# A hybrid decoder layer in split fp32: four plain blocks in place of six ahead of the Strassen pairs, token blocks made on demand, and mixer weights split by a copy and an adding transfer

## The chip, the core and the metric

The kernel runs on one core of a Trainium2 chip. The metric is device time in microseconds of one execution. TensorE (PE in the rows) multiplies, VectorE (DVE) and ScalarE (ACT) work element by element, SyncE (SP) issues plain transfers, and GpSimd (POOL) issues those transfers that add what they bring to what is in the target.

## The reference

One layer on 512 tokens of width 1024: half a step of a SwiGLU network, a mixer (4 retention heads beside 8 heads of block attention), half a step of a second SwiGLU network. All of it is fp32.

```
x = x + 0.5 * swiglu(rms(x, ffn1_norm_w), ffn1_w_gate, ffn1_w_up, ffn1_w_down)
proj = rms(x, mix_norm_w) @ w_in                   # 1024 -> 3584
ret = rms(retention(rope(rq), rope(rk), rv)) * silu(rg) * ret_out_beta
att = rms(moba(rope(rms(aq)), rope(rms(ak)), av)) * att_out_beta
x = x + concatenate([ret, att]) @ w_out
x = x + 0.5 * swiglu(rms(x, ffn2_norm_w), ffn2_w_gate, ffn2_w_up, ffn2_w_down)
swiglu(h, g, u, d) = (silu(h @ g) * (h @ u)) @ d    # 1024 -> 2816 -> 1024
```

## The kernel before

**Split products.** Tokens stand along the free dimension (512 columns). For an fp32 product in fp32r, each operand is split into a first part `h` (rounded to fp32r) and a second part `lo` (what the rounding lost). `mm3` (L396) makes a product of three matmuls, `wh xh + wh xl + wl xh`. `split_w` (L373) brings a weight in tiles of 128x512: a load of 256 KB through SP's queue, a ScalarE copy that makes `h`, and a VectorE subtraction `raw - h` that makes `lo`. Slots for these come from rings: 12 for raw weights, 6 for first parts (`wh`), 6 for second parts (`wl`), 45 for token blocks, 98 in all.

**The networks.** `ffn` (L594) has 22 blocks of 128 hidden columns. The first `EVEN` (6) are plain: per block, gate and up each take 8 x 3 matmuls of 512 columns. The other 16 are made in 8 pairs by `hidden` (L635) through `strassen` (L516): a 2x2 Strassen scheme over two halves of the inner dimension, two output blocks, and two halves of the tokens, with 7 products of 24 matmuls for the gate and 24 for the up part, each one block of 128 weights by 256 columns. A pair needs eight loads for its four quarters, two more loads and four adding transfers for sums of quarters, four VectorE sums, and 14 splits. The down projection has 10 plain blocks and 6 pairs, in the same way.

**Token blocks.** Strassen's moving side is one of seven combinations of token quarters, for each of four pairs of input blocks. `token_blocks` (L471) makes all seven for all pairs at once, ahead of the first Strassen product. The products ask for them in the order 0, 1, 3, 4, 5, 6, 2. `weave` (L574) lets neighbouring pairs overlap in the order of the program.

**The mixer.** `proj(c)` (L758) is one projection of 128 columns out of 20 (two weight tiles, 24 matmuls of 512 columns); `values(g)` (L770) makes values for half of the heads (eight weight tiles, 96 matmuls). Around them stand gates, rope, scores, softmax and norms, all with splits of their own on ScalarE and VectorE. The output projection and the second network follow.

**The order.** Nothing is issued as it is written. `Plan` (L75) notes each operation with its tiles and what it depends on, and then goes through time with a price list: at each moment an engine that is free takes, of its operations that are ready and whose slots are free, the one with the lowest place in the program plus a delay. `DELAYS` (L53) is a list of such delays by part of the mixer. The price list counts 2000 ns for a transfer to land, `DMA_LAT` (L88). The chosen order is then fixed; on the chip each engine runs its own list in order and waits on semaphores. As all goes through one helper, each row below has line 202.

Of the kernel before, what the change touches and what calls it, by code (L numbers as in the profile page):

```python
# [42 lines left out]
EARLY = 6  # L43
WARM = 8

EVEN = 6
HALF = (22 - EVEN) // 2

PLAIN = 10
# [1 line left out]
PAIRED = (22 - PLAIN) // 2  # L51

DELAYS = {  # L53
    "att norm 0": -1252, "att norm 1": 245, "att norm 2": -377, "att norm 3": -1320,
    "att out 0 0": -73, "att out 0 1": -287, "att out 1 0": -333, "att out 1 1": 71,
    "att out 2 0": -358, "att out 2 1": -145, "att out 3 0": -9, "att parts 0": -2592,
    "att parts 1": -1912, "att parts 2": -23, "att parts 3": -314, "att raw 0": 349,
    "att raw 1": -845, "att raw 2": -1954, "att rope 0": -79, "att rope 1": -982,
# [9 lines left out]
    "proj 9": 42, "ret out 1": -203, "ret out 2": 171, "ret out 3": 80, "ret rope 0": -747,  # L68
    "ret rope 1": 30, "ret rope 3": 59, "ret scores 0": 229, "ret scores 1": -861,
    "ret scores 2": 36, "ret scores 3": 123, "values 0": 399, "values 1": 751,  # L70
}
PIECES = {0: 1, 1: 2, 2: 4, 4: 8}

# [1 line left out]
class Plan:  # L75
# [9 lines left out]
           "DVE": {"PE": 260.0, "POOL": 205.0, "DVE": 130.0, "ACT": 130.0},  # L85
           "POOL": {"PE": 260.0, "POOL": 105.0}, "DMA": {}}
    LAT_ANY = {"PE": 200.0, "ACT": 145.0, "DVE": 145.0, "POOL": 100.0, "DMA": 100.0}
    LAT_FREE, DMA_LAT, WINDOW = 290.0, 2000.0, 900  # L88

    class _Engine:  # L90
        def __init__(self, plan, name, real):
# [122 lines left out]
    def _order(self):  # L214
# [25 lines left out]
        while done < n:  # L240
            progress = True
            while progress:
                progress = False
                for e in engines:
                    if busy[e] > t:
                        continue
                    skipped, pick = [], None
                    while ready[e]:
                        p, i = heapq.heappop(ready[e])
                        if i > first + self.WINDOW:  # L250
                            heapq.heappush(ready[e], (p, i))
                            break
                        if at[i] <= t:
                            new = [x for x in ops[i][4] if x not in live]
                            want = {}
                            for x in new:
                                for k in self.tiles[x]:
                                    want[k] = want.get(k, 0) + 1
                            if all(free[k] >= v for k, v in want.items()):
                                pick = i  # L260
                                for x in new:
                                    live.add(x)
                                for k, v in want.items():
                                    free[k] -= v
                                break
                        skipped.append((p, i))
                    for s in skipped:
                        heapq.heappush(ready[e], s)
                    if pick is not None:
                        progress = True  # L270
                        order.append(pick)
                        busy[e] = t + ops[pick][1]
                        if ops[pick][7]:
                            other = "POOL" if e == "DVE" else "DVE"
                            busy[e] += max(0.0, share[other] - t)
                            share[e] = busy[e]
                        end = busy[e] + (self.DMA_LAT if e in ("DMA", "POOL") else 0.0)
                        heapq.heappush(events, (busy[e], -1))
                        heapq.heappush(events, (end, pick))
            if not events:  # L280
                raise RuntimeError(f"stuck at {t}: {len(order)} of {n}: {free}")
            t, i, *x = heapq.heappop(events)
            now = [(i, x)]
            while events and events[0][0] <= t:
                _, i, *x = heapq.heappop(events)
                now.append((i, x))
            for i, x in now:
                done += self._ended(i, x, t, free, over, left, events, succ, at, need, ready)
            while first < n and over[first]:
                first += 1  # L290
# [33 lines left out]
def tile_layer(ctx: ExitStack, tc: tile.TileContext, x_t, cols_in, wg1, wu1, wd1, w_int, w_inn,  # L324
# [22 lines left out]
    def f32(ap):  # L347
        return ap.bitcast(F32)
# [21 lines left out]
            n, k = divmod(at[1], self.each)  # L370
            return self.tiles[n][:, k]

    def split_w(src, shape, pieces=None):  # L373

        each = 512 // shape[2]
        raws, hs, ls = [], [], []
        for a in range(0, shape[1], each):
# [4 lines left out]
                to.append(x)  # L382
            if pieces is None:
                nc.sync.dma_start(raw, src[:, a:a + n])
                nc.scalar.activation(h, raw, AF.Copy)
                nc.vector.tensor_sub(lo, raw, f32(h))
        if pieces is not None:
            def piece(a):
                n, o = a.start // each, slice(a.start % each, a.start % each + a.stop - a.start)
# [78 lines left out]
            nc.vector.tensor_scalar(v, ps, EPS, None, op0=OP.add)  # L468
            self.v, self.r = v, rsqrt(v)

    def token_blocks(pairs, gates=None):  # L471


        res = [[] for _ in range(7)]
        gate = lambda q: setattr(nc, "after", gates and gates[min(q, len(gates) - 1)])
        def negative(n, src, bh, bl, o):
            nc.scalar.activation(bh[:, o], src, AF.Copy, scale=-1.0)
            nc.vector.scalar_tensor_tensor(bl[:, o], src, -1.0, f32(bh[:, o]), op0=OP.mult, op1=OP.subtract)
            res[n].append((bh[:, o], bl[:, o]))

        for q, (one, two) in enumerate(pairs):
            gate(q)
            if q % 2 == 0:
                bh, bl = slot(F32R, use="block"), slot(F32R, use="block")
            negative(0, one[:, :256], bh, bl, slice(256 * (q % 2), 256 * (q % 2) + 256))

        def two_blocks(n, t):
            h, lo = split(t, use="block")
            for i in range(2):
                res[n + i].append((h[:, 256 * i:256 * i + 256], lo[:, 256 * i:256 * i + 256]))  # L490

        for q, (one, two) in enumerate(pairs):
            gate(q)
            h, lo = slot(F32R, use="block"), slot(F32R, use="block")
            nc.scalar.activation(h[:, :256], two[:, :256], AF.Copy)
            nc.vector.tensor_sub(lo[:, :256], two[:, :256], f32(h[:, :256]))
            res[1].append((h[:, :256], lo[:, :256]))
            negative(2, two[:, 256:], h, lo, slice(256, 512))
        later = []
        for q, (one, two) in enumerate(pairs):  # L500
            gate(q)
            t = slot(use="block")
            nc.vector.tensor_sub(t[:, :256], one[:, 256:], one[:, :256])
            nc.vector.tensor_sub(t[:, 256:], two[:, 256:], t[:, :256])
            two_blocks(3, t)
            u = slot(use="block")
            nc.vector.tensor_sub(u[:, :256], one[:, 256:], two[:, 256:])
            nc.vector.tensor_sub(u[:, 256:], two[:, :256], t[:, 256:])
            later.append(u)
        for q, u in enumerate(later):  # L510
            gate(q)
            two_blocks(5, u)
        nc.after = None
        return res

    def strassen(load, units, moving, taken):  # L516

# [76 lines left out]
    def ffn(st, x, wg, wu, wd, nxt, was, first=None, last=False):  # L594
# [30 lines left out]
        for q in range(4):  # L625
# [4 lines left out]
                                               op0=OP.mult, op1=OP.mult)  # L630
                two.append(t)
            pairs.append(two)
        blocks = token_blocks(pairs)

        def hidden(one, two):  # L635
            def load(queue, t, m, i, j):
# [58 lines left out]
                mm3(p, wh[:, fb], wl[:, fb], *parts[fb], fb == 0, fb == PLAIN - 1)  # L695
            nc.vector.scalar_tensor_tensor(y, p, 0.5, y, op0=OP.mult, op1=OP.add)
        units = [(n, k0, 0) for k0, n in ((k, min(4, PAIRED - k)) for k in range(0, PAIRED, 4))]
        blocks = token_blocks([(hs[PLAIN + k], hs[PLAIN + PAIRED + k]) for k in range(PAIRED)])

        def output(db):  # L700
            def load(queue, t, u, i, j):
# [55 lines left out]

    def proj(c):  # L758
        was, nc.part = nc.part, f"proj {c}"
        wh, wl = split_w(w_int[c], (128, 8, 128))  # L760
        p = bank("p")
        for kb in range(KB):
            xh, xl = s2.parts[kb]
            mm3(p, wh[:, kb], wl[:, kb], xh, xl, kb == 0, kb == KB - 1)
        nc.part = was
        return p
# [3 lines left out]
    def values(g):  # L770
# [1 line left out]
        nc.part = f"values {g}"  # L772
        ps = [bank("t") for _ in range(3)] + [bank("o")]
        for c in range(4):
            wh, wl = split_w(w_inn[4 * g + c], (128, 2, 512))
            for a in range(2):
                kb = 2 * c + a
                xh, xl = s2.parts[kb]
# [359 lines left out]
```

## Time and profile before

| | |
|---|---|
| median of 3 runs | 961.61 us (960.72 to 962.21) |
| the profiled execution | 962.12 us, span 960.4 us |
| TensorE, VectorE, ScalarE, POOL busy | 949.8, 740.9, 546.9, 83.7 us |
| plain blocks of network 1, its Strassen pairs, its down projection | to 74, to 238, to 346 us of the span |
| mixer | 346 to 577 us |
| output projection and plain blocks, Strassen pairs and down projection of network 2 | to 680, to the end |

Times in a row are from the start of the span. Busy time of TensorE holds waits that lie under the modelled end of a matmul; its pace (the time of a long run over its matmuls) says more.

### The profile page before, as it was taken

How to read it: one execution, taken by the hardware profiler on the slowest of the kernel's cores; microseconds unless marked ns; L12 is line 12 of the kernel's file. 1: busy time of each engine (PE TensorE's matmuls, PEld its weight loads, DVE VectorE, ACT ScalarE, POOL GpSimd, SP SyncE). 2: the span in 40 equal slices, each digit the busy share in tenths (PEclk: the TensorE clock that was granted, in tenths of full speed). 3: DMA queues.
4: the chain of work that ended last, by engine and by line, in shares of the span. 5: the costliest groups of instructions: out<-in, count | busy, mean ns of one | idle time of the engine just before them, and what ended most of it. 6: DMA issues, size and time to landing. Idle time of an engine off the chain costs nothing.

```text
span 960.4 us, 16972 instructions
## 1 busy us (share of the span) xinstructions
PE 949.8 (99%) x6042; PEld 857.3 (89%) x6042; DVE 740.9 (77%) x1512; ACT 546.9 (57%) x1107; POOL 83.7 (9%) x100
## 2 busy tenths in 40 slices
PE   9999999999999999999999999999999999999998
PEld 5889999999889998888788878888999999988998
DVE  7986777798836884379989998888567789893675
ACT  7544555577334555368987975554455647652341
POOL 0211111110002000000000010001111111000120
PEclk9999999999999999999999999999999999999999
DMA  9937666566438772214405554744677665563581
GB/s 310 285 89 183 182 173 154 144 149 180 157 92 186 218 256 105 64 60 121 158 24 155 173 138 109 248 115 101 155 177 180 161 167 138 154 192 99 127 200 43
DMA packets 89156, 146.95 MB, mean 153 GB/s; under 512 B 10736, under 2 KB 24816, under 8 KB 89072
## 3 DMA queue, kind: packets, MB, share of 16 engines
q1 hardware_dynamic: 75248, 122.80, 40.0%
q0 software_dynamic: 13824, 23.07, 15.1%
q8 instruction: 47, 0.77, 0.3%
q14 instruction: 37, 0.30, 0.1%
HBM read 136.40 MB, written 6.29 MB: 149 GB/s over the span
## 4 chain that ended last, share of the span: by engine, by line
PE 86%; ACT 6%; DVE 4%; DMA 1%; SPq 1%; issue 1%; DVEq 0%; ACTq 0%
PE ps L202 86%; ACT s L202 6%; DVE s L202 4%; SPq L202 1%; DMA s<-in_x_t_dram 1%; DMA s<-in_w_int_dram 0%; DMA s<-s 0%; DVE c L202 0%; DVE ad L202 0%; ACT c L202 0%; DVEq L202 0%; ACTq L202 0%
## 5 line engine op out<-in xcount | busy, mean ns | idle before, releaser
L202 PE MATMUL ps<-s 128*128 128x256 f32 (+2 forms) x5872 | 934.9, 320 | 4.6 <-ACT s L202 2.7
L202 PEld LDWEIGHTS ps<-s 128*128 128x128 f32 x5872 | 837.6, 190 | 88.1 <-ACT s L202 7.3
L202 DVE TENSOR_TENSOR s<-s 128x512 fp32r<-128x512 f32 (+4 forms) x918 | 524.6, 622 | 100.0 <-ACT s L202 94.5
L202 ACT ACTIVATE s<-s 128x512 fp32r<-128x512 f32 (+3 forms) x808 | 420.9, 577 | 268.0 <-DVE s L202 191.8
L202 DVE TENSOR_TENSOR s<-ps,s 128x256 f32<-128x256 f32 (+6 forms) x184 | 91.7, 519 | 47.5 <-PE ps L202 30.1
L202 ACT ACTIVATE s<-ps 128x512 f32<-128x512 f32 (+7 forms) x148 | 75.7, 519 | 80.9 <-PE ps L202 76.5
L202 POOL DMA_DIRECT2D s<-in_wg_dram x32 | 28.0, 875 | 575.2 <-ACT s L202 241.6
L202 DVE SCALAR_TENSOR_TENSOR s<-ps,s 128x256 f32<-128x256 f32 (+1 forms) x72 | 34.8, 483 | 38.6 <-PE ps L202 38.5
L202 POOL DMA_DIRECT2D s<-in_wd_dram x32 | 27.9, 982 | 220.6 <-PE ps L202 144.8
L202 DVE SCALAR_TENSOR_TENSOR s<-s 128x256 fp32r<-128x256 f32 (+1 forms) x70 | 37.2, 537 | 11.7 <-ACT s L202 11.4
L202 DVE SCALAR_TENSOR_TENSOR s<-s,cols 128x512 fp32r<-128x512 f32 (+1 forms) x44 | 32.1, 749 | 6.1 <-ACT s L202 5.9
L202 POOL DMA_DIRECT2D s<-in_wu_dram x32 | 29.4, 919 | 53.1 <-DMA s<-in_wu_dram 27.6
L202 ACT ACTIVATE s<-s,cols 128x512 fp32r<-128x512 f32 x24 | 17.1, 720 | 23.3 <-DVE s L202 21.3
L202 ACT ACTIVATE s<-s,c 128x384 f32<-128x384 f32 (+3 forms) x32 | 20.7, 649 | 1.6 <-DVE c L202 1.5
L202 PE MATMUL ps<-ct,s 128*128 128x128 f32 x100 | 17.3, 278 | 1.3 <-ACT s L202 1.2
L202 PEld LDWEIGHTS ps<-ct,s 128*128 128x128 f32 x100 | 11.8, 140 | 5.5 <-ACT s L202 3.9
L202 DVE CUSTOM_DVE_ANT_0 s<-ps,s 128x384 f32<-128x384 f32 (+3 forms) x32 | 14.8, 485 | 0.5 <-PE ps L202 0.4
L202 ACT ACTIVATE s<-ps,cols 128x512 f32<-128x512 f32 x8 | 5.5, 684 | 16.3 <-PE ps L202 16.3
L202 DVE TENSOR_TENSOR s<-s,ps 128x256 f32<-128x256 f32 x32 | 12.0, 417 | 0.0
L202 PE MATMUL ps<-s,cr 128*128 128x512 f32 x30 | 11.7, 410 | 0.2 <-ACT s L202 0.2
L202 DVE SCALAR_TENSOR_TENSOR s<-ps,c,s 128x128 fp32r<-128x128 f32 (+1 forms) x24 | 8.2, 389 | 1.7 <-ACT s L202 1.7
L202 DVE SCALAR_TENSOR_TENSOR s<-s,ps 128x512 f32<-128x512 f32 x12 | 8.2, 683 | 0.6 <-PE ps L202 0.6
(33 smaller groups left out, 76.9 us busy)
## 6 DMA issues: line engine op xcount, KB each, us to landing
s<-in_wg_dram SPq DMA_DIRECT2D x103, 256.0 KB, 3.5
s<-in_wu_dram SPq DMA_DIRECT2D x103, 256.0 KB, 3.6
s<-in_wd_dram SPq DMA_DIRECT2D x72, 256.0 KB, 3.1
s<-in_w_int_dram SPq DMA_DIRECT2D x40, 256.0 KB, 4.4
s<-in_wg_dram POOLq DMA_DIRECT2D x32, 256.0 KB, 4.8
s<-in_wu_dram POOLq DMA_DIRECT2D x32, 256.0 KB, 5.9
s<-in_wd_dram SPq DMA_DIRECT2D x56, 128.0 KB, 2.8
s<-in_x_t_dram SPq DMA_DIRECT2D x16, 256.0 KB, 4.9
```

Of the source, the lines that this page charges most:

```text
L202: self.ops.append([eng, cost, lambda: fn(*args, **kwargs), deps, tiles, i + self.delay + DELAYS.get(self.part, 0), self.part, shared])
```

## The change

`EVEN` goes from 6 to 4, so each network has 4 plain blocks and 9 Strassen pairs. `TokenBlocks` takes the place of `token_blocks`: it makes a block when a product first indexes it, inside the product's loop and thus behind that product's first weight split in the program. In `proj` and `values`, `split_w` gets `by="copy"`: `h` by a VectorE copy, `lo` by ScalarE as `-h`, and then an adding transfer of the same weight from memory on POOL's queue. `w_out` and the networks keep the old split. The planner prices the landing of a POOL transfer at 3000 ns, and `DELAYS` has new numbers (the first lines are shown).

```diff
-EVEN = 6
+EVEN = 4
 HALF = (22 - EVEN) // 2
...
 DELAYS = {
-    "att norm 0": -1252, "att norm 1": 245, "att norm 2": -377, "att norm 3": -1320,
+    "att norm 0": -2603, "att norm 1": 330, "att norm 2": -243, "att norm 3": 188,
...
-    LAT_FREE, DMA_LAT, WINDOW = 290.0, 2000.0, 900
+    LAT_FREE, DMA_LAT, WINDOW = 290.0, {"DMA": 2000.0, "POOL": 3000.0}, 900
...
-                        end = busy[e] + (self.DMA_LAT if e in ("DMA", "POOL") else 0.0)
+                        end = busy[e] + self.DMA_LAT.get(e, 0.0)
...
-    def split_w(src, shape, pieces=None):
+    def split_w(src, shape, pieces=None, by=None):
...
                 nc.sync.dma_start(raw, src[:, a:a + n])
-                nc.scalar.activation(h, raw, AF.Copy)
-                nc.vector.tensor_sub(lo, raw, f32(h))
+                if by == "copy":
+                    nc.vector.tensor_copy(h, raw)
+                else:
+                    nc.scalar.activation(h, raw, AF.Copy)
+                if by is None:
+                    nc.vector.tensor_sub(lo, raw, f32(h))
+                else:
+                    nc.scalar.activation(lo, f32(h), AF.Copy, scale=-1.0)
+                    nc.gpsimd.dma_start(lo, src[:, a:a + n], accum_op=OP.add)
...
-    def token_blocks(pairs, gates=None):
...
+    class TokenBlocks:
+        def __init__(self, pairs):
+            self.pairs, self.made, self.t, self.two = pairs, {}, [], []
+
+        def __getitem__(self, n):
+            if n not in self.made:
+                self.make(n)
+            return self.made[n]
...
+        def both(self, n, t):
             h, lo = split(t, use="block")
             for i in range(2):
-                res[n + i].append((h[:, 256 * i:256 * i + 256], lo[:, 256 * i:256 * i + 256]))
+                self.made.setdefault(n + i, []).append(tuple(x[:, 256 * i:256 * i + 256] for x in (h, lo)))
+
+        def make(self, n):
+            if n == 0:
+                self.made[0] = []
+                for q, (one, two) in enumerate(self.pairs):
+                    if q % 2 == 0:
+                        tiles = slot(F32R, use="block"), slot(F32R, use="block")
+                    self.made[0].append(self.one(one[:, :256], tiles, 256 * (q % 2), -1.0))
+            elif n in (1, 2):
+                if not self.two:
+                    self.two = [(slot(F32R, use="block"), slot(F32R, use="block")) for _ in self.pairs]
+                self.made[n] = [self.one(two[:, 256 * n - 256:256 * n], tiles, 256 * n - 256, 3.0 - 2 * n)
+                                for tiles, (one, two) in zip(self.two, self.pairs)]
+            elif n in (3, 4):
+                for one, two in self.pairs:
+                    t, u = slot(use="block"), slot(use="block")
+                    nc.vector.tensor_sub(t[:, :256], one[:, 256:], one[:, :256])
+                    nc.vector.tensor_sub(t[:, 256:], two[:, 256:], t[:, :256])
+                    self.both(3, t)
+                    nc.vector.tensor_sub(u[:, :256], one[:, 256:], two[:, 256:])
+                    nc.vector.tensor_sub(u[:, 256:], two[:, :256], t[:, 256:])
+                    self.t.append(u)
+            else:
+                for u in self.t:
+                    self.both(5, u)
...
-        blocks = token_blocks(pairs)
+        blocks = TokenBlocks(pairs)
...
-        blocks = token_blocks([(hs[PLAIN + k], hs[PLAIN + PAIRED + k]) for k in range(PAIRED)])
+        blocks = TokenBlocks([(hs[PLAIN + k], hs[PLAIN + PAIRED + k]) for k in range(PAIRED)])
...
-        wh, wl = split_w(w_int[c], (128, 8, 128))
+        wh, wl = split_w(w_int[c], (128, 8, 128), by="copy")
...
-            wh, wl = split_w(w_inn[4 * g + c], (128, 2, 512))
+            wh, wl = split_w(w_inn[4 * g + c], (128, 2, 512), by="copy")
```

## Rows read from the trace of the kernel before

**Rows 1.** The page: busy time, share, instructions; then transfer rate by slice.

```profile
PE 949.8 (99%) x6042; PEld 857.3 (89%) x6042; DVE 740.9 (77%) x1512; ACT 546.9 (57%) x1107; POOL 83.7 (9%) x100
...
GB/s 310 285 89 183 182 173 154 144 149 180 157 92 186 218 256 105 64 60 121 158 24 155 173 138 109 248 115 101 155 177 180 161 167 138 154 192 99 127 200 43
```

**Rows 2.** TensorE in order of time: start, us, first form's name, count of all.

```profile
24.39 85.81 PE L202 MATMUL ps<-s 128*128 128x512 f32 x519
...
580.71 44.41 PE L202 MATMUL ps<-s 128*128 128x512 f32 x195
...
625.42 74.75 PE L202 MATMUL ps<-s 128*128 128x512 f32 x408
...
699.76 132.88 PE L202 MATMUL ps<-s 128*128 128x256 f32 x1106
```

**Rows 3.** Busy us (instructions) by stretch: PE, PEld, DVE, ACT, POOL; clock; transfer share; GB/s.

```profile
27.30:66.40 39.10, 39.10 (x174) 32.36 (x174) 39.01 (x76) 21.60 (x42) 7.60 (x9) 1.00 0.60 172
74.00:238.00 164.00, 163.31 (x1353) 162.78 (x1353) 130.00 (x253) 97.20 (x190) 22.51 (x26) 1.00 0.64 164
346.00:424.00 78.00, 78.00 (x375) 65.54 (x376) 40.69 (x79) 39.34 (x72) 0.00 (x0) 1.00 0.34 118
424.00:510.00 86.00, 84.33 (x445) 70.02 (x444) 76.90 (x185) 70.96 (x159) 0.00 (x0) 1.00 0.35 107
510.00:577.00 67.00, 65.67 (x350) 54.08 (x349) 64.12 (x164) 55.55 (x129) 3.50 (x4) 1.00 0.53 150
```

**Rows 4.** TensorE's groups of one form from 424 to 577 us.

```profile
L202 PE MATMUL ps<-s 128*128 128x512 f32 x442 | 118.2, 400 | 0.5 <-DVE s L202 0.4
L202 PE MATMUL ps<-s 128*128 128x256 f32 x104 | 20.0, 292 | 0.5 <-DVE s L202 0.3 <-ACT s L202 0.2
L202 PE MATMUL ps<-ct,s 128*128 128x128 f32 x96 | 16.7, 278 | 1.3 <-ACT s L202 1.2
L202 PE MATMUL ps<-s 128*128 128x128 f32 x70 | 12.1, 252 | 0.0
L202 PE MATMUL ps<-s 128*128 128x384 f32 x40 | 11.6, 359 | 0.5 <-ACT s L202 0.3 <-DVE s L202 0.2
L202 PE MATMUL ps<-s,cr 128*128 128x512 f32 x18 | 7.2, 415 | 0.2 <-ACT s L202 0.2
L202 PE MATMUL ps<-cr,s 128*128 128x2 f32 x23 | 2.8, 235 | 0.0
```

**Rows 5.** The chain that ended last, from 424 to 577 us, by line.

```profile
by line: ACT s L202 35.1%; PE ps L202 30.1%; DVE s L202 20.7%; SPq L202 4.1%; issue 3.7%; DMA s<-in_w_int_dram 2.9%; DMA s<-s 1.5%; DVE c L202 0.8%; DVE ad L202 0.8%; ACT c L202 0.5%; DVEq L202 0.1%; ACTq L202 0.0%
```

**Rows 6.** VectorE: four pieces in order of time, and one group of one form.

```profile
46.70 0.42 DVE L202 SCALAR_TENSOR_TENSOR s<-s 128x256 fp32r<-128x256 f32 x1
47.04 0.42 DVE L202 TENSOR_TENSOR s<-s 128x256 fp32r<-128x256 f32 x1
...
617.75 4.30 DVE L202 TENSOR_TENSOR s<-s 128x512 f32<-128x512 f32 x7
...
628.34 0.69 DVE L202 SCALAR_TENSOR_TENSOR s<-s 128x512 f32<-128x512 f32 x1 [1.43 <-ACT s L202]
...
L202 DVE MEMSET idle<- 128x256 uint32 x1 | 0.3, 272 | 0.0
```

**Rows 7.** SP's mixer weight loads after 424 us: first and last of 22.

```profile
424.04 1.05 SPq L202 DMA_DIRECT2D s<-in_w_int_dram  x2
...
505.94 1.80 SPq L202 DMA_DIRECT2D s<-in_w_int_dram  x4
```

**Rows 8.** The page's transfer queues, and POOL's issues with us to landing.

```profile
q1 hardware_dynamic: 75248, 122.80, 40.0%
q0 software_dynamic: 13824, 23.07, 15.1%
...
s<-in_wg_dram POOLq DMA_DIRECT2D x32, 256.0 KB, 4.8
s<-in_wu_dram POOLq DMA_DIRECT2D x32, 256.0 KB, 5.9
```

More of the change, by code (lines that the diff above doesn't have):

```diff
@@ L53 @@
 DELAYS = {
-    "att norm 0": -1252, "att norm 1": 245, "att norm 2": -377, "att norm 3": -1320,
[L55 to L58, printed above, removed]
[9 rows of a table removed]
-    "proj 9": 42, "ret out 1": -203, "ret out 2": 171, "ret out 3": 80, "ret rope 0": -747,
-    "ret rope 1": 30, "ret rope 3": 59, "ret scores 0": 229, "ret scores 1": -861,
-    "ret scores 2": 36, "ret scores 3": 123, "values 0": 399, "values 1": 751,
+    "att norm 0": -2603, "att norm 1": 330, "att norm 2": -243, "att norm 3": 188,
+    "att out 0 0": -554, "att out 0 1": 166, "att out 1 0": 373, "att out 1 1": -807,
+    "att out 2 0": 99, "att out 2 1": -93, "att out 3 0": -2464, "att out 3 1": -87,
+    "att parts 0": -4536, "att parts 1": -2396, "att parts 2": 423, "att parts 3": -347,
+    "att raw 0": 24, "att raw 1": -2777, "att raw 2": -2297, "att raw 3": 362, "att rope 0": -905,
[8 rows of a table added]
+    "proj 7": 255, "proj 8": 71, "ret out 0": 51, "ret out 1": -34, "ret out 2": 77,
+    "ret out 3": -30, "ret rope 0": 177, "ret rope 1": -250, "ret rope 2": 2, "ret rope 3": -234,
+    "ret scores 0": 312, "ret scores 1": -682, "ret scores 2": -8, "ret scores 3": -1191,
+    "values 0": 159, "values 1": 751,
 }
@@ L469, in stats, with one @@
             self.v, self.r = v, rsqrt(v)
-    def token_blocks(pairs, gates=None):
[L474 to L487, printed above, removed]
+    class TokenBlocks:
[5 more added lines that the diff above has]
+            return self.made[n]
+        def one(self, src, tiles, o, sign=1.0):
+            h, lo = (t[:, o:o + 256] for t in tiles)
+            if sign > 0:
+                nc.scalar.activation(h, src, AF.Copy)
+                nc.vector.tensor_sub(lo, src, f32(h))
+            else:
+                nc.scalar.activation(h, src, AF.Copy, scale=-1.0)
+                nc.vector.scalar_tensor_tensor(lo, src, -1.0, f32(h), op0=OP.mult, op1=OP.subtract)
+            return h, lo
+        def both(self, n, t):
@@ L488, in two_blocks @@
             h, lo = split(t, use="block")
             for i in range(2):
-                res[n + i].append((h[:, 256 * i:256 * i + 256], lo[:, 256 * i:256 * i + 256]))
[L492 to L514, printed above, removed]
+                self.made.setdefault(n + i, []).append(tuple(x[:, 256 * i:256 * i + 256] for x in (h, lo)))
[20 more added lines that the diff above has]
+                    self.t.append(u)
+            else:
+                for u in self.t:
+                    self.both(5, u)
```

17 rows, old and new, of the table DELAYS are left out of this document.

## The prediction

> **What bounds the kernel now.** I read the page's table of engines first, then TensorE's and VectorE's instructions in order of time, then busy times by stage, and last the chain of waits and the transfers in the mixer.
>
> The table says TensorE is busy 949.8 of 960.4 us [rows 1]; VectorE is next with 740.9. But ends of matmuls are modelled, so the reader should look at the pace. In one long run of the plain form, 195 matmuls of 512 columns take 44.41 us [rows 2]; less the tail of the last (0.39), that is 44.02 / 194 = 0.227 us each. In one long run of Strassen products, 1106 matmuls of 256 columns take 132.88 us; less a tail of 0.28, that is 0.120 each. Both forms run back to back for tens of microseconds: there TensorE alone sets the time, and what is taken from it is gained in full, as long as nothing else falls behind.
>
> The same rows date the first Strassen product. From 24.39 on, 519 matmuls take 85.81 us [rows 2]. With n plain ones, 0.227 n + 0.120 (519 - n) = 85.5, so n = 217 and the first product starts near 24.4 + 49.3 = 73.7 us. For the second network 408 matmuls in 74.75 us from 625.42 give 238 plain ones and a first product near 679.5.
>
> Only the mixer wastes TensorE time. From 424 to 577 it waits visibly for 1.67 + 1.33 = 3.0 us [rows 3], and more lies under modelled ends. Counting forms there [rows 4]: 460 matmuls of 512 columns at 0.227 are 104.4, 104 of 256 at 0.120 are 12.5, 40 of 384 about 7.0 (half-way), 166 of 128 columns between 11.1 (the line through the two prices) and 19.9 (as for 256), 23 tiny ones at most 2.8. That is 135 to 147 us in 153: 6 to 18 us are lost. VectorE is busy 76.9 of 86 and 64.1 of 67 us there, ScalarE 71.0 and 55.6 [rows 3], and of the chain that ended last 35% is ScalarE, 30% TensorE, 21% VectorE [rows 5]. So both small engines share that bound, ScalarE somewhat more.
>
> **The change part by part.**
>
> **Two plain blocks become one pair**, in each network. Removed: 2 x 48 = 96 matmuls of 512 columns, 96 x 0.2269 = 21.78 us. Added: 7 products x 2 x 4 x 3 = 168 of 256 columns, 168 x 0.1200 = 20.16 us. Gain 1.62 us each, 3.25 us in both networks. This is the firm term: the pace of both forms is measured where nothing else binds. The side costs of one more pair: VectorE loses 8 splits and 6 row operations (14 x 0.602 = 8.4 us, a 512-wide pass being (4.30 - 0.69) / 6 = 0.602 [rows 6]) and gains 14 splits, 4 sums, 8 passes of 256 columns and one more of 512 (19 x 0.602 + 8 x 0.34 = 14.1 us). That extra 5.7 us lies in the Strassen stage, where VectorE is busy 130 of 164 us [rows 3]; if that cover were gone, TensorE would wait for the excess. ScalarE (97 of 164) has more room. Transfers: 10 loads through SP's queue and 4 adding ones through POOL's for 8 loads; POOL works 22.5 of 164 us.
>
> **Token blocks on demand.** This removes no work. It moves the block operations from ahead of all Strassen weights to beside the product that first needs them, so in each engine's order they fall between the weight splits. It matters since the first product now comes 96 x 0.227 = 21.8 us sooner: at 51.9 us in the first network. Before, VectorE was busy 39.01 of the 39.10 us from 27.3 to 66.4 [rows 3], and had finished 7 us ahead of that product. Of these 39.0 us, two plain blocks' work goes (8.4 us) and the block that only the last product needs may come late (4 x 0.34 = 1.3 us; a 256-wide pass is 47.04 - 46.70 = 0.34 [rows 6]). By the fifth product, which starts 4 x 24 x 0.12 = 11.5 us after the first, at 63.4, it must also have made 8 more weight splits and 4 sums (12 x 0.602 = 7.2) and 2 small sums (0.7). Needed: 39.0 - 8.4 - 1.3 + 7.9 = 37.2 us; there are 63.4 - 27.3 = 36.1. So it is late by about 1.1 us, and that then falls on TensorE. I charge 1.0 us; bounds 0 (it also idles some before 27.3, and orders can differ) and 3 (the hand-over to ScalarE and back adds to each split). In the second network the matching operation starts at 628.3 [rows 6], and the fifth product is due at 679.5 - 21.8 + 11.5 = 669.2: 40.9 us for the same 37.2, so nothing is lost. The loads for the first pair come 21.8 us sooner too; the 16 transfer engines are busy 0.60 there [rows 3], so they fit.
>
> **Weights in the mixer.** 56 tiles change: 20 projections and 8 value blocks with two each. First part: a VectorE copy in place of a ScalarE one. Second part: ScalarE writes the negated first part, and an adding transfer puts the weight on top, in place of a VectorE subtraction. ScalarE's count stays. VectorE swaps a 0.602 us pass for a copy. The trace has no 512-wide copy within SBUF. Below it cannot be under 0.272, a memory-set of 256 columns; above it is the 0.602 of the subtraction [rows 6]. The nearest row by columns read is a two-source pass of 256, which also reads 512: 0.335. So a tile saves 0.267 us of VectorE, between 0 and 0.33.
>
> [...]
>
> Where does the saving count? From 346 to 424 TensorE is busy 78.00 of 78.00 us and VectorE 40.7 [rows 3]: nothing to win there. After 424 there are 22 tiles (from 424.04 to 505.94, 22 loads [rows 7]), so VectorE gets 22 x 0.267 = 5.9 us back in a stretch where it is one of two bounds. The bounds of the gain are 0 (ScalarE holds the chain) and 22 x 0.33 = 7.3. I take half of 5.9, **2.9 us**, since ScalarE has the larger share of the chain. After 510 no weight of this kind is loaded, and that stretch is only started earlier. The new start delays are a re-ordering of the mixer's parts; I price them at nothing, within the same bounds.
>
> What is queued behind: each tile now needs load, copy, negation and adding transfer before its first product. An adding transfer takes 4.8 to 5.9 us to land [rows 8], and POOL, idle from 346 to 510, issues it in some 0.9 us. Second parts have a ring of 6 tiles, and a projection eats one per 12 x 0.227 = 2.72 us, so 16 us pass around the ring; about 7 us of latency and 2.7 of use fit in it.
>
> **Sum.** Profiled execution 962.12 (span 960.4 and 1.7 around it) - 3.25 + 1.0 - 2.9 = 957.0; the median of the runs is 0.5 below the profiled one: **956.4 us**.
>
> **The rivals.**
> *A: the mixer gives nothing.* ScalarE already holds 35% of the chain, and its count is unchanged; a copy at 0.602 would do it too. Then 961.6 - 3.25 + 1.0 = 959.4. Against it: VectorE is at 89 to 96% there, too near full not to hold anything.
> *B: VectorE was the true bound* and each saved microsecond shows: 961.6 - 3.25 + 1.0 - 5.9 = 953.5. For it: the losses of 6 to 18 us leave room. Against: VectorE is only 21% of the chain.
> *C: the adding transfers come late* (the slower side). A plain load costs 40.0% x 960.4 / 122.80 = 3.13 us of the 16 engines per MB, an adding one 15.1% x 960.4 / 23.07 = 6.29 [rows 8]. One tile of 0.262 MB thus costs 0.82 + 1.65 = 2.47 us of them, against the 2.72 us in which TensorE eats it: 91% with nothing else moving. From 10% over this price TensorE waits in the stretch around 330 to 424, where it now never does. At 2.85 us a tile, 34 tiles lose 34 x 0.13 = 4.4 us, and with nothing won elsewhere the time is 959.4 + 4.4 = 963.8. Against it: in the second slice of the page, from 24 to 48 us, they moved 285 GB/s while TensorE ran on [rows 1, 2], and a share is packet time, not a hard limit.
> [...]
> *D: the swap's gain is eaten at the start.* VectorE is late by 3 us and not 1.0, in the first network, and the second is no better than even: 957.0 - 0.5 + 2.0 = 958.4 with the mixer's gain, 961.4 without it, which is no change.
>
> **How the numbers follow.** A difference under 0.2% (1.9 us) cannot be told from no change here. Forecast 0.45, with a range of its own of 954.5 to 958.5; A 0.20 (958.3 to 961.4); B 0.14; C 0.12; D 0.09. Faster means under 959.7: the forecast, B, two thirds of A and half of D, 0.76. Slower means over 963.5: C, 0.11. The rest, 0.13, is the same. The range goes from 951.5 (B with a copy at its lower bound and no delay at the start) to 962.0, which leaves out C and little else.
>
> **What would show it.** Right: 6042 + 144 = 6186 matmuls, paces of 0.227 and 0.120 unchanged, the first Strassen product near 52 us, gaps of about 1 us among the first five products; a copy group of 56 at about 0.33 to 0.4 us; POOL with 64 more transfers; a stretch from values to out that is some 3 us shorter. Wrong: TensorE gaps between 330 and 424 or behind transfers from the mixer's weights (C); copies of 0.6 us, or a mixer as long as before with ScalarE nearly full (A); gaps over 3 us near 52 to 66 us (D). I would be wrong most easily by the re-ordering of the mixer, which I could not price from rows.

## The result and the profile after

The changed kernel takes 974.8 us (median of 4 runs, 972.25 to 976.49) against 961.53: a ratio of 1.0138, 95% interval 1.0125 to 1.0150. It is 13.3 us slower; forecast was 956.4 us, and faster. The profiled execution took 974.1 us with a span of 972.3.

The page's busy line, and the queues in transfers (columns as in [rows 1] and [rows 8]):

```profile
PE 950.6 (98%) x6186; PEld 863.6 (89%) x6186; DVE 738.7 (76%) x1538; ACT 557.0 (57%) x1127; POOL 140.3 (14%) x164
...
q1 hardware_dynamic: 75824, 123.85, 39.8%
q0 software_dynamic: 23040, 39.86, 25.3%
...
s<-in_w_int_dram POOLq DMA_DIRECT2D x40, 256.0 KB, 5.7
...
s<-in_w_inn_dram POOLq DMA_DIRECT2D x16, 256.0 KB, 7.1
...
saved<-s SPq DMA_DIRECT2D x8, 256.0 KB, 10.4
s<-s SPq DMA_DIRECT2D x16, 128.0 KB, 3.6
...
s<-s SPq DMA_DIRECT2D x32, 32.0 KB, 3.1
```

The counts are as forecast: 6186 matmuls, 164 instructions on POOL. New is the last column. Second parts take 5.7 and 7.1 us to land, and the small on-chip copies (`s<-s`, those of key halves and of rope) take 3.6 and 3.1 us; before, these were at 2.3 and 1.9.

Where the time went shows in TensorE's instructions in order of time:

```profile
24.48 85.79 PE L202 MATMUL ps<-s 128*128 128x512 f32 x604
...
344.35 7.66 PE L202 MATMUL ps<-s 128*128 128x256 f32 x57 [0.71 <-DVE s L202]
354.53 3.69 PE L202 MATMUL ps<-s 128*128 128x512 f32 x9 [2.52 <-DMA s<-in_w_int_dram]
358.53 1.67 PE L202 MATMUL ps<-s 128*128 128x512 f32 x6 [0.30 <-DMA s<-in_w_inn_dram]
...
483.53 5.48 PE L202 MATMUL ps<-s 128*128 128x512 f32 x18 [3.60 <-DMA s<-in_w_int_dram]
...
541.28 3.99 PE L202 MATMUL ps<-s 128*128 128x128 f32 x19 [2.91 <-ACT s L202]
```

The first row is unbroken, and by the prediction's equation it holds 122 plain matmuls: the first Strassen product starts at 24.5 + 122 x 0.227 = 52.2 us, and TensorE never stops there. The second row ends network 1, and the others are the mixer: TensorE stands still for a second part that has not landed (354.5, 483.5) and for ScalarE (541.3). ScalarE had itself waited for an on-chip copy of a key half, issued behind those of rope, as the chain that ended last has it:

```profile
534.15 6.37 DMA s<-s
540.60 0.64 ACT s L202
```

After the first stop TensorE is slow for some time: 9 matmuls in 3.69 us, where 9 at the 0.227 us of the networks would take 2.0.

Busy time by stretch, in the columns of [rows 3]:

```profile
27.30:66.40 39.10, 39.10 (x229) 34.77 (x228) 38.90 (x76) 24.10 (x48) 8.89 (x10) 1.00 0.78 201
...
346.00:424.00 78.00, 75.17 (x349) 62.11 (x348) 29.49 (x71) 37.02 (x68) 25.42 (x29) 0.98 0.91 218
424.00:510.00 86.00, 80.83 (x413) 66.43 (x412) 67.86 (x173) 66.54 (x150) 14.18 (x16) 0.98 0.64 155
510.00:577.00 67.00, 61.81 (x332) 51.03 (x331) 56.89 (x150) 53.67 (x124) 13.33 (x15) 1.00 0.70 162
```

and of TensorE alone around the first stop (busy, clock, transfer share, GB/s):

```profile
352.00:354.00 2.00, 0.01 (x1) 1.00 1.10 260
354.00:356.00 2.00, 1.47 (x5) 0.80 1.11 262
356.00:358.00 2.00, 2.00 (x6) 0.50 1.11 262
358.00:360.00 2.00, 1.70 (x7) 0.85 1.10 261
```

Beside [rows 3] the three mixer rows show what changed. VectorE's load fell from 76.9 to 67.9 and from 64.1 to 56.9 us, as meant, yet ScalarE's fell too, from 71.0 to 66.5 and from 55.6 to 53.7: both wait. The transfer engines went from 0.34, 0.35 and 0.53 to 0.91, 0.64 and 0.70, and around the first stop they are at 1.10 to 1.11. The granted clock drops to 0.50 behind a stop in which TensorE did nothing for 2.5 us. It did the same behind the 3.6 us before 483.5 (0.72, 0.50 and 0.92 in the six us from 484 on), but not behind the 2.9 us before 541.3 (1.00 throughout). What the clock lacks in these rows, (1 - clock) times their length, adds up to 1.7 us at either place, an estimated 3.4 us in all.

### The profile page after: what moved, and what is told of

It is laid out like the page before. It is cut to its first block, busy times and chain, and to the rows that moved or that the text cites. A ratio compares the mean times of both kernels' runs of the same rounds, so it can differ in the third digit from the quotient of the medians.

```text
span 972.3 us, 17523 instructions
## 1 busy us (share of the span) xinstructions
PE 950.6 (98%) x6186; PEld 863.6 (89%) x6186; DVE 738.7 (76%) x1538; ACT 557.0 (57%) x1127; POOL 140.3 (14%) x164
## 3 DMA queue, kind: packets, MB, share of 16 engines
q0 software_dynamic: 23040, 39.86, 25.3%
HBM read 154.22 MB, written 6.29 MB: 165 GB/s over the span
## 4 chain that ended last, share of the span: by engine, by line
PE 84%; DMA 5%; DVE 4%; issue 3%; ACT 3%; SPq 1%; POOL 0%; DVEq 0%; POOLq 0%; ACTq 0%
PE ps L202 84%; DVE s L202 3%; ACT s L202 3%; DMA s<-s 2%; DMA s<-in_w_int_dram 1%; SPq L202 1%; DMA s<-in_w_inn_dram 1%; DMA s<-in_x_t_dram 1%; DMA s<-in_wd_dram 0%; POOL s L202 0%; DVE ad L202 0%; DVE c L202 0%; DVEq L202 0%; POOLq L202 0%; ACTq L202 0%
## 5 line engine op out<-in xcount | busy, mean ns | idle before, releaser
L202 PEld LDWEIGHTS ps<-s 128*128 128x128 f32 x6016 | 843.3, 191 | 93.6 <-ACT s L202 11.2
L202 ACT ACTIVATE s<-s 128x512 fp32r<-128x512 f32 (+4 forms) x820 | 427.8, 577 | 279.6 <-DVE s L202 186.6
L202 DVE TENSOR_TENSOR s<-s 128x512 fp32r<-128x512 f32 (+4 forms) x882 | 499.8, 620 | 97.7 <-ACT s L202 92.7
L202 POOL DMA_DIRECT2D s<-in_wg_dram x36 | 32.0, 888 | 359.8 <-DVE s L202 108.1
L202 POOL DMA_DIRECT2D s<-in_w_int_dram x40 | 37.1, 1058 | 141.1 <-ACT s L202 113.3
L202 POOL DMA_DIRECT2D s<-in_wu_dram x36 | 35.2, 978 | 37.5 <-DMA s<-in_wu_dram 28.3
L202 DVE CAST s<-s 128x512 fp32r<-128x512 f32 x56 | 22.1, 426 | 0.1
L202 ACT ACTIVATE s<-s,c 128x128 f32<-128x128 f32 (+3 forms) x32 | 20.7, 649 | 0.1
L202 POOL DMA_DIRECT2D s<-in_w_inn_dram x16 | 14.6, 1034 | 38.9 <-ACT s L202 33.8
L202 DVE CUSTOM_DVE_ANT_0 s<-ps,s 128x128 f32<-128x128 f32 (+3 forms) x32 | 14.9, 486 | 0.4 <-PE ps L202 0.4
```

The lines of the kernel that those rows point to most:

```text
L202: self.ops.append([eng, cost, lambda: fn(*args, **kwargs), deps, tiles, i + self.delay + DELAYS.get(self.part, 0), self.part, shared])
```

## The experiments

Each time is a median of at least four runs; the kernel before was at 961.5 to 961.7 in every group. **Theory**: the adding transfers fill the transfer engines, so second parts and rope's copies land late. **Rivals**: the new order of the mixer, the longer chain of a tile, VectorE copies that hold POOL back.

### The parts alone

*The swap alone*: the kernel before with these lines and the class `TokenBlocks`, which is not shown again:

```diff
-EVEN = 6
+EVEN = 4
...
-        blocks = token_blocks(pairs)
+        blocks = TokenBlocks(pairs)
```

> The kernel before with four plain blocks and token blocks on demand alone; its mixer, delays and landing price stay. Theory (the loss is all in the mixer's transfers): 961.5 - 3.25 = 958.3 us, and the mixer as long as before, since nothing in it changed. Rival (the networks' part of the change also costs something that the longer trace hides, such as waits at the first products): 960 us or more, with gaps of TensorE between 52 and 66 us.

959.12 us, ratio 0.9973 (0.9962 to 0.9985). The theory's 958.3 is missed by 0.8, and TensorE runs through from 29.7 to 110.2 us without a gap, which speaks against the rival. This is the fastest version here, and it beats both kernels.

*The swap with blocks ahead*: `EVEN = 4` and nothing else.

> The kernel before with four plain blocks and all token blocks made at once as before. Theory (blocks on demand are what lets four plain blocks pay, as VectorE is full up to the first product, now at 52 us): TensorE gaps of 3 to 8 us in all at the first products of the first network, and 961 to 967 us. Rival (the planner puts blocks in time anyway): 958 to 960 us, like the swap with blocks on demand.

969.04 us, 9.9 slower than with blocks on demand and outside the range expected. TensorE in order of time:

```profile
29.63 23.54 PE L202 MATMUL ps<-s 128*128 128x512 f32 x106
58.65 51.63 PE L202 MATMUL ps<-s 128*128 128x256 f32 x415 [5.48 <-DVE s L202]
```

The first product comes 5.5 us late, for VectorE, and the mean granted clock of the run is 0.996, where the swap alone has 1.00. Blocks on demand are what makes the swap pay.

*The mixer alone*: the changed kernel with six plain blocks and `token_blocks`.

> The changed kernel with six plain blocks and all token blocks at once as before: only the mixer's weights, the delays and the landing price are new. Theory (the mixer alone loses about 15 us): 961.5 + 14.9 = 976.4 us. Rival (the delays were made for the start that four plain blocks give, and the two parts do not add up): anything more than 4 us away from it.

976.38 us, ratio 1.0158 (1.0142 to 1.0174): the loss is the mixer's, and the parts add up (976.4 + 959.1 - 961.5 = 974.0).

### Order or transfers

*No adding transfer*: the subtraction comes back, from the copied first part.

```diff
-                if by is None:
+                if by is None or by == "copy":
                     nc.vector.tensor_sub(lo, raw, f32(h))
```

> The changed kernel without the 56 adding transfers: the first part stays a VectorE copy, the second part is VectorE's subtraction again, and ScalarE is left out of the split. Order settings stay those of the change. Theory (the adding transfers crowd the 16 engines): no TensorE wait on a weight transfer is left, the share of the transfer engines from 346 to 400 falls from about 1 to under 0.5, and the time is 958 to 964 us. Rival (the new delays order the mixer badly by themselves): still over 970 us, with TensorE waiting for ScalarE and VectorE instead.

965.86 us (ratio 1.0042, 1.0027 to 1.0057). TensorE waits on no weight transfer any more, but the time is 1.9 us over the theory's range and 6.7 us above the swap alone. Of these, 3.8 are found in the next run too; the other 3.0 come with the first part made by VectorE, which then makes both parts.

*The old split under the new delays*: `by="copy"` taken out of both calls.

> The changed kernel with the mixer's weights split as before (ScalarE copy, VectorE subtraction, no second transfer), but with the new delays and landing price. Theory (the order costs nothing by itself): 958 to 961 us, like the swap alone. Rival (the delays were fitted to the new split, and without it they order the mixer badly): 963 to 968 us. In the second case the new delays are a cost only together with this split, so the run with the old delays must be read beside it.

962.89 us, between the two and nearly the rival's 963: the new delays and landing price cost the old split 3.8 us over the swap alone.

*The new split under the old delays*: `DELAYS` as before.

> The changed kernel with the delays of before; adding transfers and their landing price of 3000 stay. Since the same change without the adding's surcharge stood at 965.5 and the swap alone at 959.1, 6.4 us are open. Theory (the new delays are no part of the loss; it is the second transfer as such): 972 to 978 us. Rival (the new order of the mixer costs the 6.4 us): 966 to 970 us.

982.89 us, outside both. With the new split the new delays are no loss; it needs them, by 8 us.

### One operation, the order kept

The planner prices an adding and a plain transfer alike, so these edits leave the list of every engine as it is (but for names of what a transfer reads); where the edit changes what a transfer reads, the planner was shown the old transfer.

*A plain second transfer*:

```diff
-                    nc.gpsimd.dma_start(lo, src[:, a:a + n], accum_op=OP.add)
+                    nc.gpsimd.dma_start(lo, src[:, a:a + n])
```

> The changed kernel with the second transfer of each mixer weight as a plain one, on the same POOL queue, at the same place and behind the same waits. It overwrites the second part with the whole weight, so the mixer's products are of other numbers. Theory (what an adding transfer costs the 16 engines, 6.3 us a MB against 3.1, is the load that makes landings late): landings near 5 us in place of 6 to 13 between 346 and 400, the share near 0.75, and 964 to 968 us. Rival (it is the length of the chain load, copy, negation, second transfer, whatever the second one costs the engines): 971 to 975 us, nearly nothing gained.

965.5 us: with the second transfer kept, the adding is worth 9.3 us. The share from 346 to 390 is 0.95 and not near 0.75. Landings are shorter by 1.2 to 2.6 us, but up to 400 us still 5.9 (projections) and 7.7 us (values) at the median, against 8.5 and 9.9.

*Adding in the first 24 tiles of the program alone, and in the other 32 alone* (there `== False`):

```diff
+                    nc.adds += 1
+                    more = {"accum_op": OP.add} if (nc.adds <= 24) == True else {}
-                    nc.gpsimd.dma_start(lo, src[:, a:a + n], accum_op=OP.add)
+                    nc.gpsimd.dma_start(lo, src[:, a:a + n], **more)
```

> The changed kernel with adding transfers only for the first 24 weight tiles in the program (first values, gates, first two attention pairs); the other 32 get the plain second transfer, so their products are of other numbers. Every engine's order is that of the changed kernel. All-adding gave 974.8 and all-plain 965.5. Theory (the dense first stretch, with the transfer engines full from 346 to 390, holds most of the 9.3 us): 970 to 974 us, with the first stop near 350 to 358 us as long as now (4.8 us). Rival (the bursts after 400, of four weights at a time among the rope's transfers, hold most): 965.5 to 969 us.

968.44 us.

> The mirror: plain for the first 24 tiles, adding for the other 32. Theory: 966 to 970 us. Rival: 970 to 974 us, with the stop near 474 to 484 us as long as now.

971.25 us, with the stop near 481 us still 2.85 us long. Over 965.5 that is 2.9 and 5.7 us, 8.6 of the 9.3: the parts nearly add, and the rival is right about the place. Two thirds are lost with the last 32 tiles, which are issued after 400 us; the first stop, as long as before with the first 24 alone (2.62 and 1.70 us, at a clock of 1.00), is the smaller part.

*Adding from the chip*, first with the planner's own, other order (the raw tile lives longer), then, noted with the old source, with every queue in the order of the changed kernel:

```diff
-                    nc.gpsimd.dma_start(lo, src[:, a:a + n], accum_op=OP.add)
+                    nc.gpsimd.dma_start(lo, raw, accum_op=OP.add)
```

> The changed kernel with the adding transfer reading the weight from its raw tile on the chip and not from memory again. Theory (the 16 engines' packet time is what is full, whatever they read): share from 346 to 390 still about 1 and 972 to 978 us. Rival (reading memory twice is the cost): landings near 5 us and 965 to 968 us.

966.7 us.

> Adding transfers read the weight's raw tile on the chip, and every queue keeps the order of the changed kernel (in the first such run SP's queue had 32 lines in another order, and the time was 966.7). Theory (the source matters: a second read from memory takes part in the long landings): 966 to 969 us. Rival (it was the changed order on SP's queue, rope transfers ahead of weights): 972 to 975 us.

967.59 us, so order was not the reason. The transfer share from 346 to 390 is 1.08 in both kernels; that expectation held, and the time still fell by 7.2 us. The share alone therefore does not price a transfer. Busy time from 346 to 390, and TensorE behind 480:

```profile
346.00:390.00 44.00, 39.76 (x198) 33.18 (x197) 15.50 (x36) 16.67 (x29) 14.98 (x17) 1.00 1.08 286
...
480.45 3.94 PE L202 MATMUL ps<-s 128*128 128x512 f32 x18 [0.18 <-DMA s<-s]
```

Where the share is 1.08 next to nothing is won: 198 matmuls against 195, with 286 and 285 GB/s moved. The gain comes later. The stop of 3.60 us that ended at 483.53 is here one of 0.18, and the 18 matmuls behind it take 3.94 in place of the 5.48 us in which the changed kernel's clock fell to 0.50: 5.0 of the 7.2 us.

*An eighth of each adding transfer*: 16 of 128 rows.

```diff
-                    nc.gpsimd.dma_start(lo, src[:, a:a + n], accum_op=OP.add)
+                    add = nc.tc.nc.gpsimd.dma_start
+                    nc._note("POOL", "dma_start",
+                             lambda *_, to=lo, at=src[:, a:a + n], **k: add(to[:16], at[:16], accum_op=OP.add),
+                             (lo, src[:, a:a + n]), {})
```

> The changed kernel with each adding transfer cut to 16 of the 128 rows, an eighth of its bytes, in the same order on every queue; seven eighths of the second parts lack their addition. The chain load, copy, negation, transfer is kept, its load on the transfer engines is gone. Theory (load, not the chain's length): 961 to 964 us, near the new order with the old split (962.9), and no stop of TensorE over 2 us before 390. Rival (the hop itself is too long): 968 us or more.

960.02 us, ratio 0.9985 (0.9976 to 0.9994), 14.8 us under the changed kernel and 1 under the theory's range. Chain, order, copies and negations are all still there; bytes are gone, and with them part of each cut transfer's own landing. Landings of POOL's projection transfers before and after 400 us, first in the changed kernel (duration of the issue in ns, min/median/max, then landing):

```profile
L202 POOL DMA_DIRECT2D s<-in_w_int_dram x13: 862/1214/1925, 346.9 to 399.0; - x13
...
DMA to landing us min/median/max: 4.0/8.5/12.7
...
L202 POOL DMA_DIRECT2D s<-in_w_int_dram x28: 862/865/1882, 399.0 to 553.9; - x28
...
DMA to landing us min/median/max: 3.9/5.0/11.2
```

and with 16 rows (line 396 is the same transfer):

```profile
L396 POOL DMA_DIRECT2D s<-in_w_int_dram x14: 767/1035/1592, 346.1 to 398.1; - x14
...
DMA to landing us min/median/max: 2.3/4.8/7.2
...
L396 POOL DMA_DIRECT2D s<-in_w_int_dram x26: 767/770/1547, 400.3 to 539.2; - x26
...
DMA to landing us min/median/max: 2.3/2.6/6.0
```

Transfers that keep all their bytes land sooner too: SP's loads of projection weights and the copies of key halves and of rope, in the changed kernel (the copies are shown above) and with 16 rows:

```profile
s<-in_w_int_dram SPq DMA_DIRECT2D x40, 256.0 KB, 9.1
```

```profile
s<-in_w_int_dram SPq DMA_DIRECT2D x40, 256.0 KB, 5.3
...
s<-s SPq DMA_DIRECT2D x16, 128.0 KB, 2.4
...
s<-s SPq DMA_DIRECT2D x32, 32.0 KB, 2.0
```

So it is the load that delays others, and not only the longer landing of the adding transfers themselves. How much of the 14.8 us goes either way no run separates.

The same three kernels in small: busy time from 346 to 390 and 390 to 577 us, in the columns of [rows 3], of the changed kernel,

```profile
346.00:390.00 44.00, 41.17 (x195) 33.89 (x194) 15.29 (x35) 17.39 (x30) 14.99 (x17) 0.96 1.08 285
390.00:577.00 187.00, 176.64 (x897) 145.68 (x896) 138.95 (x356) 139.84 (x311) 37.94 (x43) 0.99 0.67 153
```

of the plain second transfer,

```profile
346.00:390.00 44.00, 41.97 (x205) 34.87 (x205) 15.18 (x35) 18.20 (x31) 10.56 (x19) 1.00 0.95 320
390.00:577.00 187.00, 182.36 (x934) 151.43 (x933) 147.12 (x373) 146.49 (x325) 23.42 (x41) 0.99 0.56 156
```

and of the 16 rows:

```profile
346.00:390.00 44.00, 42.77 (x207) 35.72 (x206) 15.38 (x36) 18.77 (x34) 15.19 (x19) 1.00 0.69 221
390.00:577.00 187.00, 184.34 (x951) 152.08 (x949) 151.78 (x387) 148.30 (x330) 32.72 (x41) 1.00 0.44 113
```

With less on the transfer engines VectorE and ScalarE do more in the same time, since they wait less: 139.0, 147.1, 151.8 us of VectorE in the second stretch.

### Remedies and the other rival

*Half the tiles added*: every other tile gets VectorE's subtraction.

```diff
+        add = by is not None
-                if by is None:
+                if not add or a // each % 2:
                     nc.vector.tensor_sub(lo, raw, f32(h))
```

> The changed kernel with adding transfers for every other weight tile of a projection or value block (28 in place of 56); the other tiles get VectorE's subtraction from the copied first part. Theory (the loss comes where the transfer engines are full, so it falls by much more than half when they are no longer full): share from 346 to 390 near 0.75, no stop of TensorE over 2 us before 390, and 963 to 967 us, about what no adding transfer at all gave (965.9). Rival (each adding transfer costs a fixed 0.2 us through its longer chain): half-way between 965.9 and 974.8, so 969 to 972 us.

965.23 us, as the theory has it: going from 28 additions to 56 costs 9.6 us, and 28 cost nothing against no addition at all. But the share from 346 to 390 is 0.83, a stop of 2.1 us remains before 353.7, and the order differs, so this supports and does not prove.

*A landing price of 9000, and a ring of 10 for second parts*:

```diff
-    LAT_FREE, DMA_LAT, WINDOW = 290.0, {"DMA": 2000.0, "POOL": 3000.0}, 900
+    LAT_FREE, DMA_LAT, WINDOW = 290.0, {"DMA": 2000.0, "POOL": 9000.0}, 900
```

> The changed kernel with 9000 in place of 3000 as the planner's price of a landing on POOL's queue, so that it asks for second parts earlier. Theory (the transfer engines are full from 346 to 390 and landings stretch to 7 to 13 us; the order was laid out for 4): waits of TensorE on weight transfers shrink from 7.8 us to under 3, and the time falls to 966 to 971 us; the full engines remain, so it does not reach 959. Rival (only throughput counts, nothing can be asked for earlier as the rings are full): 973 to 976 us.

973.18 us. TensorE's waits on weight transfers vanish, but those on ScalarE grow from 7.6 to 11.5 us. The rival's time, and neither's mechanism: the waits moved from weights to ScalarE. That the same bytes, asked for earlier, delay something else would fit, and is not shown.

> The changed kernel with 10 slots for second parts in place of 6. Theory (in the two dense stretches the engines' throughput limits, not the number of slots): 972 to 976 us, with shares of the transfer engines still about 1 from 346 to 386. Rival (six slots are too few for a landing of 6 to 13 us, so the next transfer is issued too late): TensorE's waits on weight transfers vanish and the time is under 968 us.

973.47 us with the same order on every engine, and TensorE's waits on weight transfers are still 7.3 us; the theory holds.

*The first part by ScalarE*:

```diff
-                if by == "copy":
+                if by == "never":
                     nc.vector.tensor_copy(h, raw)
```

> The changed kernel with the first part made by ScalarE as before, and the adding transfer kept, so VectorE does nothing for a mixer weight and ScalarE 56 x 0.52 = 29 us more. Theory (VectorE's copies are harmless to POOL; the transfers set the loss): POOL's issues as long as now (1.05 us mean), 974 to 980 us, since ScalarE is fuller. Rival (the VectorE copies hold POOL back): issues near 0.88 us, landings shorter, and under 972 us.

973.81 us. POOL's issues are as short as the rival said (0.88 us), and the time is not: whatever lengthened them is not the loss. Nor do the rows point to the copies. In the changed kernel (VectorE, then POOL, in order of time),

```profile
347.14 1.27 DVE L202 CAST s<-s 128x512 fp32r<-128x512 f32 x3
...
377.00 1.42 DVE L202 CAST s<-s 128x512 fp32r<-128x512 f32 x4
```

```profile
346.92 1.79 POOL L202 DMA_DIRECT2D s<-in_w_int_dram  x2 [21.55 <-ACT s L202]
348.76 1.75 POOL L202 DMA_DIRECT2D s<-in_w_inn_dram  x2
349.83 1.57 POOL L202 DMA_DIRECT2D s<-in_w_int_dram  x1
...
378.56 0.86 POOL L202 DMA_DIRECT2D s<-in_w_inn_dram  x1 [6.07 <-ACT s L202]
379.10 3.00 POOL L202 DMA_DIRECT2D s<-in_w_int_dram  x3
```

an issue that follows closely starts before the one ahead of it has ended (the second at 347.45, the first ends at 347.83), so its time (1.26 us) overlaps that one's. Taken as runs, the five issues beside copies go from 346.92 to 351.40, 0.90 us each, and the four with no VectorE instruction beside them from 378.56 to 382.10, 0.89 each; a lone one takes 0.86. POOL's pace is the same with copies and without. That VectorE's copies hold POOL back is not borne out by these rows.

## Why the prediction was wrong

**The swap, -3.25 + 1.0.** Right in the sum: measured -2.6 (959.12 against 961.68 in the same group), forecast -2.25. Its parts show in TensorE's order of time, before and with the swap alone:

```profile
227.52 117.60 PE L202 MATMUL ps<-s 128*128 128x256 f32 x764 [0.69 <-ACT s L202]
...
833.33 123.87 PE L202 MATMUL ps<-s 128*128 128x256 f32 x816 [0.69 <-ACT s L202]
```

```profile
225.29 117.61 PE L202 MATMUL ps<-s 128*128 128x256 f32 x764 [0.69 <-ACT s L202]
...
579.08 44.38 PE L202 MATMUL ps<-s 128*128 128x512 f32 x195
...
830.07 123.87 PE L202 MATMUL ps<-s 128*128 128x256 f32 x816 [0.69 <-ACT s L202]
```

Network 1 is 1.6 us shorter (227.52 - 24.39 against 225.29 - 23.75, where 24.39 [rows 2] and 23.75 start the unbroken run of its blocks), network 2 another 1.6 (833.33 - 580.71 [rows 2] against 830.07 - 579.08): the gain is as forecast. The 1.0 us for VectorE's backlog is not seen, with VectorE full (38.90 of 39.10 us) and TensorE unbroken. Instead the stretch between them, mostly the mixer, is 0.6 us longer, ordered anew around the same delays. That the sum came out is in part luck.

**Blocks on demand.** Their reason was right and their worth unpriced: without them the swap turns from a gain of 2.6 us into a loss of 7.6.

**The price of the copy.** Right: four casts in a row (the row at 377.00) take 1.42 us, so with 0.42 for one they step by (1.42 - 0.42) / 3 = 0.33 us, where I took 0.335 from a 256-wide pass.

**The mixer's gain of 2.9, and the new delays at nothing.** No gain over the swap alone was found: 960.0 with 16 rows is 0.9 above it. But two things lie in that number. With the old split the new delays stand at 962.9, so they are not free: they cost 3.8 us there. The new split with an eighth of the bytes is 2.9 below that. The orders of these two kernels differ, so whether VectorE's freed time is worth 2.9 us or nothing, as in rival A, stays open.

**The step that failed** is the one that looks at the ring alone: 16 us pass around it and about 7 us of latency fit, so the second transfer costs nothing. I took landings of 4.8 to 5.9 us from the networks, where the transfer engines stand at 0.64. In the mixer from 346 to 390 they stand at 1.08, against 0.45 before, because of the very transfers being priced, and landings are 8.5 us at the median, 12.7 at most. They queue: the five issued from 346.92 to 349.83 land after 7.6, 9.0, 9.7, 11.2 and 12.7 us, one every 2.0 us. Even 12.7 and 2.7 of use fit in 16, and a ring of 10 changed little; it is the conclusion that does not follow. In place of nothing, the runs show 14.8 us (974.8 - 960.0): 5.5 for moving the weights a second time, 9.3 for adding. So the steps from 959.1 are + 3.8 (delays) - 2.9 (split, an eighth of the bytes) + 5.5 + 9.3 = 974.8.

**Rival C** named the mechanism and had the engine time right (25.3% x 972.3 / 39.86 = 6.17 us a MB, forecast 6.29), but its price of 4.4 us was a third of the loss. It counted only TensorE's need of tiles before 424. Missing were the clock at 0.50 behind two of the stops (an estimated 3.4 us), and above all what else uses the engines: two thirds of the adding's cost lie after 400 us, where weights share them with the copies of rope and key halves, and those take 3.6 and 3.1 us to land, against 2.3 and 1.9. I had even written there that the share "is packet time, not a hard limit", and read it as comfort.

**What stays open.** That adding from memory costs this kernel 7.2 us more than adding from the chip was shown, most of it at one stop near 481, and why was not. Nor is it known how much of the late loss runs through rope's copies and how much through weights, since no run moved the one without the other.

## What to carry to other kernels

A transfer that takes work off a compute engine is priced with the load that it makes: put its packet time on top of the share of the stretch where it will run, take landings from a stretch that is as full, and let transfers that are queued land one after the other (here 2.0 us apart, at 256 KB and a share of 1.08). Ask who else has transfers in a chain there, and whether they wait on the chip's own copies. To test such a change, keep the order and cut the bytes: one run with an eighth of the rows told what the bytes cost from what the longer chain costs.

## What the hardware showed that was not expected

At an equal transfer share of 1.08 from 346 to 390, adding from an on-chip tile and adding from memory gave 967.6 and 974.8 us, by what came later; five queued adding transfers of 256 KB from memory landed 2.0 us apart. Of plain ones queued at the same place, at a share of 0.95, the first and the third let TensorE go on at 353.70 and 356.43 us, 1.4 us a transfer. And back-to-back issues on POOL show up to 1.9 us each, while their pace is 0.89 us, next to 0.86 for a lone one.
